# The first normalization of a hybrid encoder block: scaling by diagonal matrices on TensorE, with a fixed TensorE order at the start

## The chip, the cores and the metric

The kernel runs on one core of a Trainium2 chip. The metric is device time in microseconds (us), a median over runs. The engines are named as in the profile: PE is TensorE's matmul, PEld its weight load, DVE is VectorE, ACT is ScalarE, POOL is GpSimd, and SP is the queue that issues most DMAs.

## What is computed

One layer of a hybrid encoder works on 1024 frames of 1024 features, all in float32. The change touches the first of its three parts, and the third part in passing:

```python
x = x + 0.5 * swiglu(rmsnorm(x, ffn1_norm), ffn1_w_gate, ffn1_w_up, ffn1_w_down)   # first FFN, width 2816
h = rmsnorm(x, mix_norm); p = h @ w_in                                             # gMLP and gated DeltaNet
x = x + concat(A, B) @ w_out
x = x + 0.5 * swiglu(rmsnorm(x, ffn2_norm), ffn2_w_gate, ffn2_w_up, ffn2_w_down)   # second FFN
y = rmsnorm(x, final_norm)

rmsnorm(x, g) = x * rsqrt(mean(x * x) + 1e-6) * g        # mean over the 1024 features of a frame
swiglu(x, ...) = (silu(x @ w_gate) * (x @ w_up)) @ w_down
```

## The kernel before

**Precision.** Every operand of a product is split into a rounded high part and a remainder (`split`: ACT makes the high part, DVE or POOL subtracts it from the source), and a product of two split operands is three matmuls (`mm3`: high by high, high by low, low by high).

**Layout.** `x` is loaded in eight tiles of 128 frames (`xs[0]` to `xs[7]`). For the first products the features must lie on the partitions, so that each tile of frames is transposed on TensorE. The hidden width of 2816 is worked through in 22 chunks of 128 columns of the gate and of the up matrix.

**Seven products for eight.** Chunks 1 to 21 (`gu`) multiply 2 by 2 blocks in Winograd's scheme: with the transposed activations as blocks B11, B12, B21 and B22 (frames 0 to 511 or 512 to 1023, features 0 to 511 or 512 to 1023) and their sums T1 to T4, seven products of 12 matmuls each do for eight. The sums T1 to T4 come from DVE and POOL. Chunk 0 (`gu_plain`) uses the plain eight products, since the sums are not there yet. It runs in two halves: 256 columns of frames of each block, then the other 256. In each half it makes 96 matmuls of 256 columns: gate and up, two frame blocks, and two feature blocks of four 128-feature steps `k`.

**The start (`start1`).** For each tile ACT squares and sums, DVE and POOL make the reciprocal root, and DVE scales the tile by it and by the gain `g`, which was broadcast to all partitions by a DMA (`grow`, line 66). TensorE transposes the scaled tile four 128-column pieces at a time into a PSUM bank (`transposed`, line 95), and ACT and DVE take from the bank the high part, the low part and the sums (`blocks`, lines 118 to 150). The first four tiles (0, 4, 1, 5) feed the first half of chunk 0 and the other four (2, 6, 3, 7) the second half. The weight pieces of a chunk come by `load_gu` (SP's queue, line 185), and their sums (line 191) are POOL's.

**Order.** A scheduler orders the instructions of every engine from the program; each engine then works its list strictly in order, and waits where a semaphore is missing. PSUM has two pools of four banks, `mm` (`A`) and `ax` (`X`). In the start the transposes take `ax`, and chunk 0's four accumulators take `mm`. `weight_sums(q)` (line 278) prepares sums of the down matrix for the later product; it is called once every two chunks, from chunk 1 on, and its work is DMA and POOL.

**The second FFN** uses the same `gu_plain`, `gu` and `blocks`. Its norm gain is broadcast by the same `grow`, into one buffer that all four gains share in turn.

Of the kernel before, what the change touches and what calls it, by code (L numbers as in the profile page):

```python
# [17 lines left out]
P = 128  # L18
# [12 lines left out]
def block_kernel(ctx: ExitStack, tc, a, out):  # L31
# [75 lines left out]
    class Combos:  # L107
        def __init__(self, g, qp, bp):
            self.g, self.qp, self.bp, self.B, self.f = g, qp, bp, {}, {}

        def put(self, n, i, src, eng):
# [5 lines left out]
            t = self.B[n][:, :, :, i * P:i * P + P]  # L117
# [34 lines left out]

        def put_sums(self, i, names, engs):
# [11 lines left out]
    def ffn(cb, wgu, wd, ps, rp, gp, qp, bp, start, load_xts, emit, before={}, fill=None):  # L165
# [63 lines left out]
        def gu_plain(sl, b12):  # L229
# [81 lines left out]
        for c in range(1, NCH):  # L311
            together(load_gu(c))
            if c % 2:
                weight_sums(c // 2)
            else:
# [129 lines left out]
    ba = cp.tile([P, 16, 8], F32, tag="ba", name="ba")[:, :8]  # L445
# [9 lines left out]
    xs = load_x(xdram, (0, 4))  # L455
    g = grow("ffn1_norm")
    xs.update(load_x(xdram, (1, 5)))

    with ExitStack() as f1:
# [5 lines left out]
        cb = Combos(g, qp, bp)  # L465

        def start1(f):
            def xi(i):
                return xs[i], xs[i + 4]

            uv = [cb.sums() for _ in range(2)]
            for j in range(2):
                for i in range(2):
                    normed(xi(i)[j], g, xi(i)[j], uv[i][j])
# [3 lines left out]
            weights = f.load_gu(0, True)  # L478
            next(weights)
            xs.update(load_x(xdram, (2, 6, 3, 7)))  # L480
            b = b12()
            parts = [cb.blocks(i, f.X, xi(i), uv[i], b) for i in range(2)]
            together(*parts, n=2)
            together(*parts, weights)
            rest = xi(2) + xi(3)
            ms = sm.tile([P, 4], F32, tag="ssk", name="ms4")
            for i, x in enumerate(rest):
                nc.scalar.activation(f.gtile(F32, "junk").rearrange("p s n -> p (s n)"), x, AF.Square, accum_out=ms[:, i:i + 1])
            rs = sm.tile([P, 4], F32, tag="rk", name="rs4")
            nc.vector.tensor_scalar(rs, ms, 1.0 / D, EPS, op0=ALU.mult, op1=ALU.add)  # L490
            rpow(rs, rs, 4)
            for i, x in enumerate(rest):
                nc.vector.scalar_tensor_tensor(x, x, rs[:, i:i + 1], g, op0=ALU.mult, op1=ALU.mult)
            f.gu_plain(slice(0, 256), b)
            b = b12()
            for i in range(2, 4):
                together(cb.blocks(i, f.X, xi(i), cb.sums(xp), b))
            f.gu_plain(slice(256, 512), b)
            V, G = nc.vector, nc.gpsimd
            together(*(cb.put_sums(i, ("T2", "T1", "T3", "T4"), (V, G, V, G)) for i in range(4)))  # L500
# [42 lines left out]
        ffn(cb, a["f1gu"], a["f1wd"], ps, rp, gp, qp, bp, start1, load_xts, to_mid, {2: [after]}, z0)  # L543
# [14 lines left out]
    with ExitStack() as f2:  # L558
# [37 lines left out]
        cb = Combos(g2, qp, bp)  # L596
# [710 lines left out]
```

## Time and profile before

| | before |
|---|---|
| median of 3 runs | 1849.43 us (1847.9, 1849.43, 1852.1) |
| the profiled execution's own time | 1841.22 us |
| its span, first to last instruction | 1839.4 us |
| PE busy | 1784.1 us, 97% |
| DVE, ACT and POOL busy | 65%, 37%, 41% |
| PE busy from 0 to 60 us | 39.2 us |

The span is what the trace covers; 1.8 us of the profiled execution lie outside it. The profiled execution was faster than the three timed runs by some 8 us, so that differences in the trace are compared with the trace, and carried to the median as differences. A chunk of `gu` takes 84 matmuls of 512 columns. "Busy" of PE is modelled from pipelined matmuls.

### The profile page before, as it was taken

Reading aid. Unit: us, or ns where it says so; the run is one execution under the profiler, and the core shown is the slowest. Engines: PE = TensorE matmul, PEld = TensorE weight load, DVE = VectorE, ACT = ScalarE, POOL = GpSimd, SP = SyncE. Lnnn points to the kernel's source line nnn. Section 1 sums busy time; section 2 is a strip of 40 time slices with the busy share of each in tenths; the row PEclk is TensorE's granted clock in tenths of the full one; section 3 lists DMA queues with packets and bytes.
Section 4 is the critical chain, followed back from the end, with each engine's and each line's share of the span. In section 5 each row is a group of like instructions: output and inputs, shape, how many; then the busy total and the mean of one; then the engine's idle time right before and its main releaser. Section 6 shows DMA issues by size and latency. Waiting matters only on the chain.

```text
span 1839.4 us, 25484 instructions
## 1 busy us (share of the span) xinstructions
PE 1784.1 (97%) x9735; PEld 1524.8 (83%) x9735; DVE 1191.7 (65%) x1531; ACT 686.6 (37%) x1193; POOL 747.9 (41%) x583
## 2 busy tenths in 40 slices
PE   5999999999999999898999999999999999999997
PEld 4888888888788889797788989988888888878886
DVE  6867676665565575769655344587776766656546
ACT  6333332333343454432344533452333323243433
POOL 4667666565140012212132420366666665614001
PEclk9999999999999999999999999999999999999999
DMA  5353443544957445453432254334535445495744
GB/s 196 108 175 136 162 152 134 184 158 163 339 188 258 155 177 164 140 195 100 133 94 67 90 197 136 109 104 165 178 132 171 144 154 188 142 344 185 264 142 149
DMA packets 134441, 302.26 MB, mean 164 GB/s; under 512 B 27408, under 2 KB 42032, under 8 KB 134320
## 3 DMA queue, kind: packets, MB, share of 16 engines
q1 hardware_dynamic: 131824, 296.20, 46.9%
q10 hardware_dynamic: 2496, 4.44, 0.8%
q8 instruction: 76, 1.25, 0.3%
q14 instruction: 45, 0.37, 0.1%
HBM read 208.83 MB, written 91.77 MB: 163 GB/s over the span
## 4 chain that ended last, share of the span: by engine, by line
PE 78%; DVE 8%; DMA 5%; POOL 4%; issue 3%; ACT 2%; SPq 0%; POOLq 0%; DVEq 0%; ACTq 0%
PE mm L53 43%; PE ax L53 32%; POOL s L191 1%; POOL t L278 1%; DMA left<-hq 1%; DVE acc L873 1%; PE ax L95 1%; PE sd L53 1%; DMA graw<-in_f1gu_dram 1%; POOL s L278 1%; PE sc L53 1%; DVE T L119 0%; DVE unit L62 0%; DVE wk L62 0%; DVE E L797 0%
## 5 line engine op out<-in xcount | busy, mean ns | idle before, releaser
L53 PE MATMUL mm<-unit 128*128 128x512 f32 x1056 | 244.9, 392 | 4.2 <-ACT unit L61 2.2
L53 PEld LDWEIGHTS mm<-unit 128*128 128x128 f32 x1056 | 198.8, 189 | 47.4 <-ACT unit L61 3.3
L191 POOL TENSOR_TENSOR s<-graw 128x512 f32<-128x512 f32 x84 | 130.3, 1551 | 262.9 <-DMA graw<-in_f2gu_dram 116.0
L62 DVE TENSOR_TENSOR ga<-graw,ga 128x512 fp32r<-128x512 f32 x134 | 155.9, 1166 | 99.9 <-ACT ga L61 99.2
L61 ACT CAST gs<-s 128x512 fp32r<-128x512 f32 x168 | 104.5, 622 | 301.8 <-PE mm L53 151.0
L62 DVE TENSOR_TENSOR unit<-left,unit 128x1024 fp32r<-128x1024 f32 x84 | 101.9, 1215 | 133.0 <-ACT unit L61 132.3
L53 PE MATMUL ax<-T,gs 128*128 128x512 f32 x792 | 183.1, 389 | 0.0
L53 PE MATMUL ax<-unit 128*128 128x512 f32 x792 | 180.5, 389 | 0.0
L53 PEld LDWEIGHTS ax<-T,gs 128*128 128x128 f32 x792 | 148.7, 188 | 30.8
L53 PEld LDWEIGHTS ax<-unit 128*128 128x128 f32 x792 | 148.7, 188 | 30.8
L62 DVE TENSOR_TENSOR gs<-s,gs 128x512 fp32r<-128x512 f32 x168 | 172.7, 1030 | 2.3
L53 PE MATMUL mm<-B,ga 128*128 128x512 f32 (+1 forms) x864 | 166.8, 347 | 3.3 <-ACT B L118 1.9
L61 ACT CAST unit<-left 128x1024 fp32r<-128x1024 f32 x84 | 82.5, 982 | 230.2 <-PE ax L53 100.5
L53 PE MATMUL mm<-T,gs 128*128 128x512 f32 x720 | 166.5, 389 | 0.0
L53 PEld LDWEIGHTS mm<-B,ga 128*128 128x128 f32 x864 | 139.5, 194 | 23.4 <-ACT B L118 2.5
L53 PEld LDWEIGHTS mm<-T,gs 128*128 128x128 f32 x720 | 135.2, 188 | 28.0
L70 POOL TENSOR_TENSOR rs<-rs,half 128x1 f32<-128x1 f32 (+1 forms) x29 | 19.2, 662 | 334.5 <-DVE rs L76 334.4
L53 PE MATMUL mm<-actT,wk 128*128 128x512 f32 x576 | 150.4, 403 | 0.0
L53 PE MATMUL ax<-B,ga 128*128 128x512 f32 x528 | 127.2, 390 | 1.4 <-DVE ga L62 1.4
L53 PE MATMUL mm<-wk,actT 128*128 128x256 f32 x960 | 123.5, 285 | 2.7 <-DVE wk L62 2.7
L53 PEld LDWEIGHTS mm<-wk,actT 128*128 128x128 f32 x960 | 117.4, 190 | 3.4 <-DVE wk L62 3.0
L53 PEld LDWEIGHTS mm<-actT,wk 128*128 128x128 f32 x576 | 103.6, 188 | 18.8
(239 smaller groups left out, 3046.0 us busy)
## 6 DMA issues: line engine op xcount, KB each, us to landing
left<-hq SPq DMA_DIRECT2D x70, 512.0 KB, 5.0
graw<-in_f1gu_dram SPq DMA_DIRECT2D x44, 512.0 KB, 5.4
wq<-t SPq DMA_DIRECT2D x44, 512.0 KB, 2.8
hq<-s SPq DMA_DIRECT2D x44, 512.0 KB, 3.1
graw<-in_f2gu_dram SPq DMA_DIRECT2D x44, 512.0 KB, 4.7
right<-wq SPq DMA_DIRECT2D x40, 512.0 KB, 4.8
wd<-in_f1wd_dram SPq DMA_DIRECT2D x22, 512.0 KB, 6.6
hq<-sg SPq DMA_DIRECT2D x22, 512.0 KB, 3.7
```

What stands on the lines that cost most here:

```text
L53: nc.tensor.matmul(*args, **kw)
L61: nc.scalar.copy(h, src)
L62: nc.vector.tensor_tensor(l, src, h, op=ALU.subtract)
L70: nc.gpsimd.tensor_tensor(o, i, half[:, :w], op=ALU.pow)
L95: nc.tensor.transpose(ps[:, i * P:(i + 1) * P], blk(i), ident)
L191: nc.gpsimd.tensor_tensor(f, u, v, op=op)
L278: nc.gpsimd.tensor_tensor(o, u, v, op=op)
L873: nc.vector.scalar_tensor_tensor(acc, pad[:, j:j + 512], cw[:, blk, j:j + 1], acc, op0=ALU.mult, op1=ALU.add)
```

## The change

1. **Norm by diagonals.** The tiles are no longer scaled. For each tile ACT squares (now with the scale 1/32 ahead of the square, so that the sum is the mean), POOL adds the epsilon and takes the power, and a 128x128 diagonal matrix `dg` of the tile's 128 factors is made from the identity (on DVE for the first four tiles, on ACT for the other four). TensorE then multiplies a piece of `x` by this diagonal in float32, which transposes and scales at once. The gain is now a column `g1` with one number per partition (a DMA of 32 bytes per partition), and is applied as ACT (`nc.scalar.mul`) and DVE (`scalar_tensor_tensor`) read the bank.
2. **TensorE order fixed.** The start stands under a manual schedule for PE. Ahead of it, 24 float32 products of the identity by itself go into a bank that nobody reads. Bank `c` now holds piece `c` of all four tiles (512 columns), so that a half needs eight banks. `gu_plain` goes step by step in `k`, and the last four banks' products stand between the first four steps. The sums T1 to T4 are cast and subtracted in pieces of 1024 elements per partition instead of 512.
3. **Weight sums later.** `weight_sums(0)` moves from chunk 1 to chunk 2, and chunk 1's weights are loaded within the start.
4. **Broadcast pinned.** The DMA of `grow` keeps its place in the program's order on ACT.

The order of the tiles changes too: 0, 1, 4, 5 and then 2, 3, 6, 7. The diff, cut:

```diff
     def grow(name):
         g = cp.tile([P, D], F32, tag="grow", name="grow")
-        nc.scalar.dma_start(g, a[name].to_broadcast([P, D]))
+        tc.keep_in_program_order(nc.scalar.dma_start(g, a[name].to_broadcast([P, D])))
         return g
...
+        def scaled_blocks(self, i, pp, xts, dg, g, f, b12, ahead):
+            sl = slice(i * 256, i * 256 + 256)
+            t3, t1, t2, t4 = self.f[i] = f
+            def less(o, src, c, v):
+                nc.vector.scalar_tensor_tensor(o, src, g[:, c:c + 1], v, op0=ALU.mult, op1=ALU.subtract)
+            def put(h, l, src, c):
+                nc.scalar.mul(h, src, g[:, c:c + 1])
+                less(l, src, c, h)
+            banks = []
+            def turn(k):
+                cs = range(len(banks), len(banks) + k)
+                banks.extend(bank(*pp) for _ in cs)
+                for n, x in enumerate(xts):
+                    for c in cs:
+                        mm(banks[c][:, n * P:n * P + P], x[:, c * P:c * P + P], dg[:, n * P:n * P + P], start=True, stop=True)
+            turn(ahead)
+            for c in range(8):
+                if c == len(banks):
+                    turn(1)
+                u, v = banks[c][:, :256], banks[c][:, 256:]
+                k = c % 4
+                if c < 4:
+                    b = self.block("B11")
+                    put(b[:, 0, k, sl], b[:, 1, k, sl], u, c)
+                    nc.scalar.mul(t3[:, k], u, g[:, c:c + 1])
+                    b = b12[k // 2]
+                    put(b[:, 0, k % 2], b[:, 1, k % 2], v, c)
+                    less(t1[:, k], v, c, t3[:, k])
+                else:
+                    b = self.block("B21")
+                    put(b[:, 0, k, sl], b[:, 1, k, sl], u, c)
+                    b = self.block("B22")
+                    put(b[:, 0, k, sl], b[:, 1, k, sl], v, c)
+                    less(t2[:, k], v, c, t1[:, k])
+                    less(t4[:, k], u, c, t2[:, k])
+                yield
...
-            for i, x in ((0, "B11"), (1, "B12"), (0, "B21"), (1, "B22")):
-                first = x[1] == "1"
-                for p, wt in ((gates[i], g["B11" if first else "a12"]), (ups[i], g["a21" if first else "a22"])):
-                    products(p, wt, xs[x], sl, first, not first)
+            for first in (True, False):
+                for k in range(4):
+                    for i, x in enumerate(("B11", "B12") if first else ("B21", "B22")):
+                        x = xs[x]
+                        for p, wt in ((gates[i], g["B11" if first else "a12"]), (ups[i], g["a21" if first else "a22"])):
+                            mm3(p, wt[:, 0, k], wt[:, 1, k], x(0, k, sl), x(1, k, sl), first and k == 0, not first and k == 3, skip_group_check=True)
+                    yield
...
+            def factors(ts, diag):
...
+                    nc.scalar.activation(junk, xs[t], AF.Square, scale=D ** -0.5, accum_out=m)
+                    nc.gpsimd.tensor_scalar(r, m, EPS, None, op0=ALU.add)
+                    rpow(r, r, 1)
+                    diag(dg[:, n * P:n * P + P], ident, r)
...
+            def plain(i, dg, fs, b, ahead, also=()):
+                bl = cb.scaled_blocks(i, f.X, [xs[t] for t in order[i]], dg, g1, fs, b, ahead)
+                together(islice(bl, 4))
+                together(also)
+                pr = f.gu_plain(slice(i * 256, i * 256 + 256), b)
+                for _ in bl:
+                    next(pr)
+                together(pr)
+            with tc.manual_schedule(engines={mybir.EngineType.PE}):
+                warm = bank(*f.X)
+                for _ in range(24):
+                    mm(warm[:, :P], ident, ident, start=True, stop=True)
...
+                plain(0, dg, four(cb.sums() + cb.sums()), b12(), 4, weights)
+                dg = factors(order[1], nc.scalar.mul)
+                t4 = rp.tile([P, 1088], F32, tag="graw", name="t4", bufs=4)[:, :D].rearrange("p (a n) -> p a n", a=2)
...
+                plain(1, dg, fs, b12(), 1)
...
+            together(f.load_gu(1), *(cb.scaled_sums(i, ("T2", "T1", "T3", "T4"), (V, G, V, G)) for i in range(2)))
```

**TensorE and DVE between the two halves of chunk 0.** The first two pieces show TensorE's list there, before and then of the change; `mm_...` are chunk 0's accumulators, `ax_...` the `ax` banks, `x_...` the tiles of frames, `dg_395` the diagonals of the second four tiles, and `ga..` weight pieces.

```order
L53 MATMUL mm_262<-B22_227,ga22_240 128x256 x11
L95 MATMUL ax_368<-ident_69,x_156 128x128 x4
L95 MATMUL ax_376<-ident_69,x_158 128x128 x4
L95 MATMUL ax_386<-ident_69,x_156 128x128 x4
L95 MATMUL ax_393<-ident_69,x_158 128x128 x4
L95 MATMUL ax_404<-ident_69,x_160 128x128 x4
L53 MATMUL mm_438<-B11_172,ga11_150 128x256
```

Of the change:

```order
L53 MATMUL mm_258<-B22_250,ga22_239 128x256 x3
L53 MATMUL ax_422<-dg_395,x_180 128x128
L53 MATMUL ax_422<-dg_395,x_182 128x128
...
L53 MATMUL ax_455<-dg_395,x_186 128x128
L53 MATMUL ax_466<-dg_395,x_180 128x128
...
L53 MATMUL ax_466<-dg_395,x_186 128x128
L53 MATMUL mm_477<-B11_214,ga11_171 128x256 x3
```

What moved: the transposes of one pair of tiles filled a bank each and freed it soon; now 16 products fill the four banks `ax_422` to `ax_455`, and the fifth, `ax_466`, takes the memory of `ax_422`, so that it and all that stands behind it wait until ACT and DVE have read `ax_422`. DVE's list at that place, of the change:

```order
L163 SCALAR_TENSOR_TENSOR f_191<-ax_317,ba_76,f_190 128x256
L209 TENSOR_TENSOR T2_624<-f_190,T2_624 128x4x256
L306 TENSOR_TENSOR sg_388<-sg_388,mm_257 128x256
L209 TENSOR_TENSOR T3_643<-f_188,T3_643 128x4x256
L306 TENSOR_TENSOR sg_388<-sg_388,mm_258 128x256
L163 SCALAR_TENSOR_TENSOR B11_214<-ax_422,ba_76,B11_214 128x256
L163 SCALAR_TENSOR_TENSOR B11_214<-ax_433,ba_76,B11_214 128x256
L163 SCALAR_TENSOR_TENSOR B12_420<-ax_422,ba_76,B12_420 128x256
L163 SCALAR_TENSOR_TENSOR f_418<-ax_422,ba_76,f_417 128x256
```

What moved: the low parts of T2 and T3 of the first half now stand ahead of the first reader of `ax_422`, of which the last, `f_418`, frees the bank. Before, the four scalings of tiles (line 493) and two products with `sg` stood there, and the low parts of the sums (line 119) came later.

**ACT and POOL at the same place,** of the change; `f_188` to `f_191` are the sums t3, t1, t2, t4 of the first half, and `rk`, `ssk` the factors.

```order
L546 ACTIVATE dg_395<-ident_69,rk_394 128x128
L208 CAST T1_634<-f_189 128x4x256
L208 CAST T2_624<-f_190 128x4x256
L208 CAST T4_654<-f_191 128x4x256
L305 ACT_TABLE_LOAD
L305 ACTIVATE sg_388<-mm_255 128x256
L208 CAST T3_643<-f_188 128x4x256
L305 ACTIVATE sg_388<-mm_256 128x256
L166 ACTIVATE B11_214<-ax_422,ba_76 128x256
```

POOL's list of the change there:

```order
L70 TENSOR_TENSOR rk_394<-rk_394,half_70 128x1
L209 TENSOR_TENSOR T1_634<-f_189,T1_634 128x4x256
L206 TENSOR_TENSOR f_188<-f_190,f_188 128x1024
L209 TENSOR_TENSOR T4_654<-f_191,T4_654 128x4x256
L209 TENSOR_TENSOR T1_634<-f_418,T1_634 128x4x256
```

What moved: ACT's cast of T3 stands ahead of its first reading of `ax_422`, and needs `f_188`, which POOL makes only after T1's low part. Before, ACT's first reading of a bank there (`f_366<-ax_368`) stood behind casts of pieces of 512 elements.

**ACT in the second FFN, ahead of the bank readings of its second half,** before:

```order
L118 CAST T4_11029<-f_10281 128x4x128
L66 DMA grow_11338<-in_final_norm_dram 128x1024
L243 ACT_TABLE_LOAD
L243 ACTIVATE sg_10837<-mm_10737 128x256
L243 ACTIVATE sg_10837<-mm_10738 128x256
L133 COPY f_10844<-ax_10846 128x512
```

Of the change:

```order
L121 CAST T4_11084<-f_10336 128x4x128
L305 ACT_TABLE_LOAD
L305 ACTIVATE sg_10892<-mm_10792 128x256
L305 ACTIVATE sg_10892<-mm_10793 128x256
L136 COPY f_10899<-ax_10901 128x512
```

What moved: the broadcast of the last gain, which waits for the last reader of the gain before it, leaves this place, and stands 52 instructions later.

## Rows read from the trace of the kernel before

**Rows 1.** The page's forty slices, busy share of PE in tenths.

```profile
PE   5999999999999999898999999999999999999997
```

**Rows 2.** Windows: stretch, length, busy PE PEld DVE ACT POOL, clock, DMA, GB/s.

```profile
0.00:60.00 60.00, 39.16 (x251) 35.87 (x252) 45.43 (x60) 37.06 (x72) 30.43 (x28) 0.89 0.43 162
30.00:40.00 10.00, 4.86 (x35) 4.48 (x34) 6.50 (x5) 4.47 (x10) 7.24 (x6) 0.84 0.15 52
40.00:50.00 10.00, 7.30 (x32) 6.23 (x31) 9.55 (x17) 7.02 (x15) 4.42 (x4) 0.50 0.37 130
50.00:60.00 10.00, 10.00 (x83) 10.00 (x83) 10.00 (x11) 5.72 (x12) 8.67 (x6) 0.98 0.12 45
```

**Rows 3.** Chain of waits, 0 to 170 us: start, length, what.

```profile
62.67 18.89 PE ax L53 x82
...
81.56 19.04 PE mm L53 x84
```

**Rows 4.** PE's timeline: start, time, engine, line, operation, tiles, shape, count, [idle before, releaser].

```profile
9.36 1.11 PE L95 MATMUL ax<-ident,x 128*128 128x128 f32 x4 [9.36 <-DVE x L82]
...
22.84 1.04 PE L95 MATMUL ax<-ident,x 128*128 128x128 f32 x8
...
36.26 0.63 PE L95 MATMUL ax<-ident,x 128*128 128x128 f32 x4 [3.56 <-DVE x L493]
38.47 2.79 PE L95 MATMUL ax<-ident,x 128*128 128x128 f32 x12 [1.58 <-DVE x L493]
...
45.87 2.80 PE L95 MATMUL ax<-ident,x 128*128 128x128 f32 x12 [0.28 <-DVE B L142]
...
50.78 1.48 PE L53 MATMUL mm<-B,ga 128*128 128x256 f32 x11
...
912.67 1.05 PE L53 MATMUL ax<-wq,ks 128*128 128x128 f32 x8
```

**Rows 5.** Groups by line and shape: count, busy us, mean ns, idle before.

```profile
L53 PE MATMUL ax<-wq,ks 128*128 128x128 f32 x64 | 8.6, 275 | 0.0
...
L95 PE MATMUL ax<-ident,oh 128*128 128x128 f32 x32 | 5.0, 280 | 0.0
...
L61 ACT CAST unit<-left 128x1024 fp32r<-128x1024 f32 x70 | 73.7, 1053 | 189.9 <-PE ax L53 79.9 <-PE mm L53 67.9 <-DMA left<-hq 31.0
...
L70 POOL TENSOR_TENSOR rs<-rs,half 128x1 f32<-128x1 f32 x28 | 18.1, 649 | 334.5 <-DVE rs L76 334.4
```

**Rows 6.** DMA issues, 0 to 24 us: KB each, us to landing.

```profile
ident<-in_cst_dram ACTq DMA_DIRECT2D x1, 64.0 KB, 4.0
```

**Rows 7.** One window of 1 us, columns as in rows 2.

```profile
3.00:4.00 1.00, 0.00 (x0) 0.00 (x0) 0.00 (x0) 0.00 (x0) 0.00 (x0) 1.00 1.06 414
```

**Rows 8.** ACT's timeline, 0 to 10 us.

```profile
0.72 0.40 ACTq L454 DMA_DIRECT2D ident<-in_cst_dram  x1
...
4.56 1.06 ACT L74 ACTIVATE f<-x 128x1024 f32<-128x1024 f32 x1 [1.64 <-DMA x<-in_x_dram]
```

**Rows 9.** DVE's timeline, 38 to 44 us.

```profile
40.64 0.74 DVE L244 TENSOR_TENSOR sg<-sg,mm 128x256 f32<-128x256 f32 x2
```

**Rows 10.** Instructions on tile graw, 0:70 us: ns min/median/max, first/last start.

```profile
L62 DVE TENSOR_TENSOR ga<-graw,ga x8: 681/1541/1780, 15.4 to 69.8; 128x512 fp32r<-128x512 f32 x8
L191 POOL TENSOR_TENSOR s<-graw x4: 1292/1459/1743, 26.1 to 67.0; 128x512 f32<-128x512 f32 x4
```

**Rows 11.** PE's timeline, 1184 to 1201 us (second FFN's start).

```profile
1185.04 1.84 PE L53 MATMUL mm<-B,ga 128*128 128x256 f32 x14
1187.53 2.90 PE L53 MATMUL mm<-B,ga 128*128 128x256 f32 x22 [0.66 <-DVE ga L62]
```

**Rows 12.** ACT's timeline, 1192 to 1201 us.

```profile
1197.47 1.28 ACT L243 ACT_TABLE_LOAD   x1 [4.73 <-DVE xn L82]
1198.77 0.66 ACT L243 ACTIVATE sg<-mm 128x256 f32<-128x256 f32 x2
1199.31 0.59 ACT L133 COPY f<-ax 128x512 f32<-128x512 f32 x1
```

More of the change, by code (lines that the diff above doesn't have):

```diff
@@ L116, in put @@
                     self.B[n] = act_tile(name=n)
-            t = self.B[n][:, :, :, i * P:i * P + P]
+            return self.B[n]
+        def put(self, n, i, src, eng):
+            t = self.block(n)[:, :, :, i * P:i * P + P]
             nc.scalar.copy(t[:, 0], src)
@@ L163, in together, with ffn @@
             pass
-    def ffn(cb, wgu, wd, ps, rp, gp, qp, bp, start, load_xts, emit, before={}, fill=None):
+    def ffn(cb, wgu, wd, ps, rp, gp, qp, bp, start, load_xts, emit, before={}, fill=None, late=0):
         A, X = (ps[0], "mm"), (ps[1], "ax")
@@ L311, in ffn @@
         for c in range(1, NCH):
-            together(load_gu(c))
-            if c % 2:
+            if c not in gu_s:
+                together(load_gu(c))
+            if c % 2 and c > late:
                 weight_sums(c // 2)
-            else:
+            elif c % 2 == 0:
+                if c // 2 * 2 == late + 1:
+                    weight_sums(0)
                 hidden_sums(c // 2 - 1)
@@ L444, in block_kernel @@
     sp = {n: dr.tile([8, P, 512], F32, tag="sp" + n, name="sp" + n) for n in "zvm"}
-    ba = cp.tile([P, 16, 8], F32, tag="ba", name="ba")[:, :8]
+    ba = cp.tile([P, 16, 8], F32, tag="ba", name="ba")
+    g1 = ba[:, 8]
+    ba = ba[:, :8]
     def load_x(src, ts):
@@ L475, in b12 @@
             def b12():
                 return [f.gtile(F32R, "B12").rearrange("p s (k n) -> p s k n", k=2) for _ in range(2)]
[L478 to L498, printed above, removed]
+            def four(ts):
+                return [t.rearrange("p a (b n) -> p (a b) n", b=2) for t in ts]
+            def plain(i, dg, fs, b, ahead, also=()):
[6 more added lines that the diff above has]
+                together(pr)
@@ new lines, in start1 @@
+            with tc.manual_schedule(engines={mybir.EngineType.PE}):
+                warm = bank(*f.X)
+                for _ in range(24):
+                    mm(warm[:, :P], ident, ident, start=True, stop=True)
+                weights = f.load_gu(0, True)
+                dg = factors(order[0], nc.vector.tensor_scalar_mul)
+                together(islice(weights, 2))
+                xs.update(load_x(xdram, order[1]))
+                plain(0, dg, four(cb.sums() + cb.sums()), b12(), 4, weights)
+                dg = factors(order[1], nc.scalar.mul)
+                t4 = rp.tile([P, 1088], F32, tag="graw", name="t4", bufs=4)[:, :D].rearrange("p (a n) -> p a n", a=2)
+                fs = four([xp.tile([P, 2, 512], F32, tag="x", name="f") for _ in range(3)] + [t4])
+                plain(1, dg, fs, b12(), 1)
@@ L626, in start2 @@
                     normed(xs[i + 4 * j], g2, xns[i][j])
-            f.gu_plain(slice(0, 256), b)
+            together(f.gu_plain(slice(0, 256), b))
             c = b12()
@@ L630, in start2 @@
                 together(cb.blocks(i, pp, xns[i], cb.sums(xp), c))
-            f.gu_plain(slice(256, 512), c)
+            together(f.gu_plain(slice(256, 512), c))
             V, G = nc.vector, nc.gpsimd
```

42 lines of the change are left out of this document (25 added, 17 removed).

## The prediction

> **What bounds the kernel now.** The first view is the page's forty slices: PE stands at 9 nearly everywhere, and only the first slice, of 46 us, is at 5 [rows 1]. So time can be won where PE is not full. The windows measure it: 39.2 us of work in the first 60 [rows 2]. The chain of waits gives the frame: from 62.67 us it is PE alone, one chunk every 19.04 us, and chunk 1 ends at 81.56 [rows 3]. Whatever the start gains must show as an earlier end of chunk 1; nothing behind it has slack to give.
>
> PE's timeline names the waits: the largest is from 32.7 to 36.26 for the scaling of the tiles on DVE (line 493), with 1.58 for the same line behind it [rows 4]. The clock costs too: the granted clock is 0.84 in 30 to 40 us, 0.50 in 40 to 50 and 0.98 in 50 to 60, that is 1.2 GHz from 3.2 us before 40 to 0.4 behind 50, 36.8 to 50.4 [rows 2]. Pace shows it: a transpose takes (1.04-0.27)/7 = 0.11 us at 22.84, and (2.79-0.42)/11 = 0.215 at 38.47 [rows 4]. The transposes at 9.36 take 1.11 for four, the slow pace too, against 0.63 at 36.26 [rows 4]. So the start is at 1.2 GHz before the change as well.
>
> **The price of a diagonal.** A float32 product that is no transpose stands in the trace as two records: the program issues 32 of `ax<-wq,ks` and the trace has 64, but of `ax<-ident,oh` it issues 32 and has 32 [rows 5]. Eight records take 1.05 us, (1.05-0.275)/7 = 0.11 each [rows 4], so that a diagonal product costs 0.22 us at 2.4 GHz where a transpose cost 0.11, and 0.43 at 1.2. The Trainium skill ("TensorE: Matmul & The Clock Gate", Terms) says of the transpose mode that it is 4 times faster for float32; by that a diagonal product would take 0.44 us, and the sum below would be 14 us longer ahead of what waits hide. I go by the rows, which have a factor of 2; rival 4 is the other case. The work of PE in the start is then 64 x 0.223 + 192 x 0.12 = 37.3 us after the 24 idle products; before it was 64 x 0.11 + 23 = 30. The 0.12 is that of eleven records at 50.78, (1.48-0.28)/10 [rows 4].
>
> **The start, step by step** (us from the span's start).
>
> *Factors.* The first tile lands at 4.5 [rows 8], and the DMAs move some 414 GB/s, 0.5 MB in 1.27 us [rows 7]. Without the broadcast of 0.5 MB the other three of the first half land by 4.5 + 3 x 1.27 = 8.3. Its square takes 1.06 [rows 8], POOL's power 0.65 [rows 5] and the add no more than that, the diagonal 0.3 on DVE (a quarter of the 0.68 of 512 columns [rows 10], and its start): the fourth diagonal is ready at 11.0 at the latest.
>
> *Idle products.* The identity lands 4.0 us after its issue [rows 6] at 0.72 [rows 8], at 4.7. 24 products at 0.43 would end at 15.0. After 36.8 the clock rose 4.5 us into the run of work that began at 45.87; so I let it rise at 9.3: 11 products before, 13 at 0.22 after, end 12.2. So it is these, not the factors, that set the first diagonal: 12.2, and 16 products fill four banks at 15.8, the first one at 15.1.
>
> *First drain.* Bank 0 needs ACT's high part (0.38), two weight casts that stand between (0.52 each, half of 1024 columns [rows 5]), t3 and B12; on DVE B11's low part, two weight low parts (0.6 each), B12's low part and t1. One 256-column reading follows the next after 0.28 on ACT (two in 0.66 [rows 12]) and 0.33 on DVE (two in 0.74 [rows 9]). That ends at 18.3; PE waits 2.5 us. Then four banks and the first 48 products, 16 x 0.223 + 48 x 0.12 = 9.35, and 48 more, 5.8: the first half ends at 33.4 (before: 32.7). ACT's squares of the last four tiles lie beside that, and DVE, with 28 readings of 0.33, keeps ahead.
>
> *Second drain.* 16 diagonals to 37.0, then `ax_466` waits for `ax_422`. ACT's chain: the last diagonal at 30.1 (square at 27.9, POOL 0.75), cast of T1 to 31.2; POOL then T1's low part and `f_188`, 2.5 us each alone (two pieces of 1.29 [rows 10], less a start); ACT casts T3 (1.05 [rows 5]); DVE T3's low part (1.2 alone), then one `sg` and four readings: 40.2. Beside each other both engines slow down: 512 elements on DVE take 0.68 alone and 1.78 beside POOL, on POOL 1.29 and 1.74 [rows 10]. With that from 32.2 on it is 42.4. The Trainium skill ("SBUF — State Buffer", Who interferes with whom) has the shared port of DVE and POOL as a lock: with two inputs in SBUF the later one waits for the whole other instruction. By that DVE would wait out three POOL instructions, and it would be 42.8; the rows agree with the size, and no run here tells a lock from a shared rate. I take 41.5, nearer the row of the pair, since most of this stretch has both at work: PE idles 4.5 us.
>
> *Second half.* 9.35 + 5.8 = 15.1 at 2.4 GHz: 56.6. A pause of 3.6 us was followed by the fall at 36.8, so I let the clock fall, and rise 4.5 us after work resumes: half of 4.5 is lost, 58.9.
>
> *Chunk 1.* Its second product needs T2's and `gs2`'s low parts. The last bank is filled 7.2 us before 58.9, eight DVE readings and a cast later T2 begins at 55.6 and ends at 56.8 alone or 59.1 beside POOL, `gs2` at 57.4 or 60.9; needed at 61.6. So no wait, and 84 x 0.227 = 19.04 ends it at 77.9. For some ten handovers from engine to engine at 0.06 each I add 0.6: 78.5 against 81.56, **3.0 us less**.
>
> **The other parts.** The first weight sums, four POOL pieces, move behind chunk 1; there POOL takes its sums for chunk 1 instead, so that I count them at nothing. Were POOL's list as full as before there, DVE's pieces would cost 1.78 for 0.68 each [rows 10], which is rival 2. In the second FFN the step-wise `gu_plain` asks for `ga21` after 3 products, not 12: PE had done 14 products when it waited for that low part until 1187.53 [rows 11], and will have done 5: 9 x 0.12 = 1.1 us more wait. The pinned broadcast pays it back: ACT stood still for 4.73 us, with that DMA's wait in its list (the order ahead of these rows), so that table load and `sg` came only at 1197.47; the first bank was read at 1199.31 [rows 12]. Without it the reading needs only its transposes, which come 0.6 later: 1199.1. What PE waits for next hangs on that reading. I count 0, bounds -0.4 and +1.1. The other orders move one DMA or two copies, with full PE over them: 0.
>
> **Sum.** -3.0 us: the trace's 1841.2 becomes 1838.2, and on the scale of the runs 1849.4 becomes 1846.4, 0.16% less. What a measurement of this kernel tells from no change is about 0.2%, 3.7 us.
>
> **Rivals.**
> 1. *The second drain is short and the clock holds.* T1 and T3 on POOL run alone (40.2), no fall, and the idle products end at 11.5: 58.9-2.25-1.3-0.7 = 54.7, chunk 1 ends at 73.7 to 76: 5 to 8 us less, 1841.4 to 1844.4. For it: POOL's shortest pieces are at 1.29, and DVE's at 0.68 [rows 10]. Against: the T2 and T3 pieces have both inputs in SBUF, as `ga` there.
> 2. *DVE bounds chunk 1.* If POOL is busy through 56 to 70, T2, `gs2`, `gs1`, T3 and `gs3` take 3.5+1.78+1.78+3.5+1.78 with two `sg` of 0.33 between, from 55.6 to 68.6 or, with a weight piece of chunk 2 between, 70; PE asks at 67.1. Chunk 1 ends at 80 to 81.5: 0 to 1.5 us less, 1848 to 1849.4. For it: DVE was the last wait before, at 62.67 [rows 3]. Against: POOL's pieces of chunk 2 need a weight load that stands behind `sg`'s store in SP's queue and takes the buffer of `t4`; until it lands POOL has little to do.
> 3. *Slower: the clock does not rise by the idle products.* Then these end at 15.0, the first bank is full 13 x 0.43 later, the first drain ends at 23.8, and with a rise 4.5 us after that the first half ends at 41.2, 7.8 later than above. Nothing behind it takes that up: chunk 1 ends at 86, 4.8 us more, 1854. It decides with the time of the rise: at 15 the gain is gone, at 25 the kernel is slower by 3.7. For it: at 9.36 to 15, before, PE ran at the slow pace with work of a microsecond at a time. Against: there it paused in between, and here it has no pause from 4.7 on.
> 4. *Slower: four passes instead of two.* At 0.44 us a diagonal product the 64 put 14 us more on PE, of which the two drains hide some 5: 6 us more than before, 1855. Against: eight records in 1.05 us. The Trainium skill ("TensorE: Matmul & The Clock Gate", Terms) has the factor of 4 that would make this so; the trace does not agree.
>
> **How the numbers follow.** Forecast (1.2 to 4.9 us less) 0.43, rival 1 0.26, rival 2 0.18, rival 3 0.08, rival 4 0.02, an unseen wait of either sign 0.03. A third of the forecast lies beyond 3.7 us: faster 0.14+0.26+0.02 = 0.42; slower 0.08+0.02+0.01 = 0.11; the same 0.47. The forecast's own range is 1844.5 to 1848.2. For 8 in 10, rival 1's end, with 1 us for the spread of the runs, gives 1840.5, and rival 2 with the upper run gives 1852.
>
> **What would show it.** In the trace after: 24 pairs of records of the identity from 4.7; their pace changing at about 9.3; first diagonal near 12.2; a wait of 2.5 us at 15.8 for DVE; a wait of 3 to 5.5 us at 37 for DVE behind T3; granted clock 0.5 for some us after it; chunk 1 ending near 78.5. The prediction is wrong if the start has another long wait, if the clock never rises before 16, or if chunk 2 waits for its weights.

## The result and the profile after

The change made the kernel slower. The median of 6 runs is 1856.88 us (1855.47 to 1863.87) against 1847.91 of the kernel before (6 runs, 1847.65 to 1852.1): ratio 1.0046, 95% interval 1.0028 to 1.0064, that is 5 to 12 us more. The forecast was 3 us less, in a range of 1840.5 to 1852.0.

The profiled execution took 1857.08 us, with a span of 1854.9. The span shown of before was 1839.4, so the traces differ by 15.5 us and the medians by 9.0. The profiled execution of before was a quick one; experiment 1 shows how much executions of one kernel differ.

The chain of waits of the kernel after, 0 to 120 us (columns as in [rows 3]):

```profile
64.47 2.49 POOL T L209
66.98 3.80 DMA graw<-in_f1gu_dram
...
75.63 0.69 DVE pe L326
...
82.10 19.04 PE mm L53 x84
```

Chunk 1 ends at 82.10, against 81.56 in [rows 3] and 78.5 forecast. So the start gained nothing, and it is no longer the product of weights that is last there, but a chain over POOL, a weight load and DVE, inside chunk 1. The page's forty slices have a 6 where [rows 1] have a 5: PE does more in the first slice, and is not done sooner.

PE's timeline of the kernel after, the start:

```profile
4.91 7.20 PE L53 MATMUL ax<-ident 128*128 128x128 f32 x48 [4.91 <-DMA ident<-in_cst_dram]
11.95 3.74 PE L53 MATMUL ax<-dg,x 128*128 128x128 f32 x32
18.35 1.92 PE L53 MATMUL ax<-dg,x 128*128 128x128 f32 x8 [2.66 <-DVE f L163]
...
27.78 7.44 PE L53 MATMUL mm<-B,ga 128*128 128x256 f32 x60
35.06 3.73 PE L53 MATMUL ax<-dg,x 128*128 128x128 f32 x32
45.60 2.05 PE L53 MATMUL ax<-dg,x 128*128 128x128 f32 x8 [6.81 <-DVE f L163]
...
76.36 3.02 PE L53 MATMUL ax<-B,gs 128*128 128x512 f32 x12 [0.17 <-DVE pe L326]
...
81.94 2.88 PE L53 MATMUL mm<-B,ga 128*128 128x512 f32 x12
```

32 records of diagonal products take 3.74 us, 0.117 each, so the price of a diagonal is as forecast. The two drains are 2.66 and 6.81 us (forecast 2.5 and 4.5). Behind each of them eight records take some 2 us, twice the 1.06 that they take later. The windows say the same: the granted clock is 0.92, 0.90 and 0.66, which is 1.6, 2.0 and 6.8 us at 1.2 GHz (for about half of the 6.8 us PE stands idle). The slow pace of the identity's first records shows in their times alone: over them the granted clock of the windows reads 1.00.

```profile
10.00:20.00 10.00, 7.34 (x60) 7.18 (x59) 5.18 (x13) 5.21 (x13) 0.65 (x2) 0.92 0.84 325
20.00:30.00 10.00, 10.00 (x80) 10.00 (x79) 6.65 (x16) 7.78 (x20) 2.35 (x6) 0.90 0.19 62
40.00:50.00 10.00, 4.40 (x24) 4.43 (x25) 7.40 (x14) 6.24 (x16) 1.86 (x1) 0.66 0.00 1
```

The second drain, in POOL's timeline of the kernel after, and then DVE's:

```profile
33.89 2.38 POOL L209 TENSOR_TENSOR T<-f,T 128x1024 fp32r<-128x1024 f32 x1 [1.45 <-ACT T L208]
36.23 3.33 POOL L206 TENSOR_TENSOR f<-f 128x1024 f32<-128x1024 f32 x1
39.53 2.34 POOL L209 TENSOR_TENSOR T<-f,T 128x1024 fp32r<-128x1024 f32 x1
```

```profile
34.79 2.56 DVE L209 TENSOR_TENSOR T<-f,T 128x1024 fp32r<-128x1024 f32 x1 [1.52 <-ACT T L208]
...
40.67 2.28 DVE L209 TENSOR_TENSOR T<-f,T 128x1024 fp32r<-128x1024 f32 x1 [2.81 <-ACT T L208]
42.87 0.41 DVE L306 TENSOR_TENSOR sg<-sg,mm 128x256 f32<-128x256 f32 x1
43.20 0.86 DVE L163 SCALAR_TENSOR_TENSOR B<-ax,ba,B 128x256 fp32r<-128x256 f32 x2
```

T1's low part, then the difference for T3 (`f`), then T3's cast on ACT, then on DVE T3's low part (40.67), and only then DVE reads the bank that PE waits for. POOL's row at 39.53 is T4's low part, DVE's at 34.79 T2's.

The second FFN, PE's timeline of the kernel after; [rows 11] have its counterpart:

```profile
1193.89 0.76 PE L53 MATMUL mm<-B,ga 128*128 128x256 f32 x5
1196.66 1.33 PE L53 MATMUL mm<-B,ga 128*128 128x256 f32 x9 [2.01 <-DVE ga L62]
1199.70 11.49 PE L53 MATMUL mm<-B,ga 128*128 128x256 f32 x82 [1.71 <-DVE x L672]
1211.04 1.91 PE L95 MATMUL ax<-ident,xn 128*128 128x128 f32 x16
...
1230.68 2.68 PE L53 MATMUL ax<-B,ga 128*128 128x512 f32 x11
```

Of the kernel before, behind the two rows of [rows 11]:

```profile
1190.58 7.46 PE L53 MATMUL mm<-B,ga 128*128 128x256 f32 x60 [0.15 <-DVE x L593]
1197.88 1.91 PE L95 MATMUL ax<-ident,xn 128*128 128x128 f32 x16
...
1218.10 2.91 PE L53 MATMUL ax<-B,ga 128*128 128x512 f32 x12
```

From the first product to the first transpose it is now 17.15 us; before it was 12.84 (1185.04 to 1197.88). The second wait was not in the forecast: behind 14 products PE asks for the fourth accumulator's bank, which DVE has not yet emptied (line 672, before 593, adds a bank of the product with `w_out` to `x`). Before, PE asked for it behind 36 products. In both kernels the bank is there 5.5 to 5.8 us after the first product (1190.58 and 1199.70), so the order costs the products that are not done by then, and the first wait lies within the second. The clock adds to it: the granted clock is 0.58 in 1199 to 1202 us and 0.85 in 1202 to 1205, which is 3.4 us at 1.2 GHz, and 1.00 there in the kernel before.

### The profile page after: what moved, and what is told of

Read it like the earlier page. It is cut to its first block, busy times and chain, and to the rows that moved or that the text cites. A ratio compares the mean times of both kernels' runs of the same rounds, so it can differ in the third digit from the quotient of the medians.

```text
span 1854.9 us, 25735 instructions
## 1 busy us (share of the span) xinstructions
PE 1800.2 (97%) x9847; PEld 1541.8 (83%) x9847; DVE 1127.6 (61%) x1542; ACT 690.3 (37%) x1205; POOL 747.3 (40%) x588
## 4 chain that ended last, share of the span: by engine, by line
PE 81%; DVE 5%; POOL 5%; DMA 4%; issue 2%; ACT 2%; SPq 0%; POOLq 0%; DVEq 0%; ACTq 0%
PE mm L53 46%; PE ax L53 32%; POOL s L250 1%; DMA left<-hq 1%; POOL t L340 1%; DVE acc L952 1%; PE ax L95 1%; PE sd L53 1%; PE sc L53 1%; POOL T L209 1%; POOL s L340 1%; POOL E L878 0%; DVE o L82 0%; DVE unit L62 0%; POOL brs L70 0%
## 5 line engine op out<-in xcount | busy, mean ns | idle before, releaser
L62 DVE TENSOR_TENSOR ga<-graw,ga 128x512 fp32r<-128x512 f32 x134 | 132.3, 990 | 122.8 <-ACT ga L61 122.5
L62 DVE TENSOR_TENSOR gs<-s,gs 128x512 fp32r<-128x512 f32 x168 | 167.4, 998 | 5.7 <-ACT gs L61 3.2
L70 POOL TENSOR_TENSOR rs<-rs,half 128x1 f32<-128x1 f32 x24 | 16.0, 665 | 323.4 <-DVE rs L76 323.3
```

What stands on the lines that cost most here:

```text
L62: nc.vector.tensor_tensor(l, src, h, op=ALU.subtract)
L70: nc.gpsimd.tensor_tensor(o, i, half[:, :w], op=ALU.pow)
```

## The experiments

Theory A: the step order in the second FFN makes some 4 us of the loss, the start is held by the chain of the second drain, and the rest differs from execution to execution. Rival B: the whole loss comes from the start, or from the stages in the middle, by the change. All ratios are to the kernel before, run on the same chip. "Chunk 2" is the start of PE's first product of chunk 2, "drain" the second drain, "FFN 2" the time there from the first product to the first transpose; all from PE's timelines.

| run | chunk 2 | drain | FFN 2 | ratio (95%) |
|---|---|---|---|---|
| before | 81.40 | | 12.84 | 1 |
| 1 before, again | 81.39 | | 12.90 | 1.0013 (0.9992 to 1.0034) |
| after | 81.94 | 6.81 | 17.15 | 1.0046 (1.0028 to 1.0064) |
| 2 after, again | 81.78 | 6.82 | 17.07 | one execution |
| 3 after, FFN 2 old | 82.89 | 6.81 | 12.92 | 1.0021 (1.0005 to 1.0036) |
| 4 before, FFN 2 new | 81.26 | | 16.95 | 1.0015 (0.9996 to 1.0034) |
| 5 = 3, T3 behind | 78.86 | 1.72 | 12.94 | 0.9975 (0.9955 to 0.9995) |
| 6 = 5, idle products in the first drain | 78.77 | 1.72 | 12.92 | 0.9973 (0.9949 to 0.9997) |
| 7 = 3, no idle products | 77.20 | 2.78 | 12.90 | one execution |
| 8 = 3, weight sums at chunk 1 | 91.34 | 6.82 | 12.96 | one execution |
| 9 = 6, reading ahead of gs | 75.73 | 1.72 | 12.88 | 0.9985 (0.9956 to 1.0014) |
| 10 = 9, 8 idle products | 71.88 | 1.46 | 13.14 | 0.9966 (0.9945 to 0.9987) |
| 11 = 10, two gs behind | 69.81 | 1.44 | 13.16 | 0.9983 (0.9965 to 1.0001) |
| 12 = after, 8 idle products | 75.28 | 3.24 | 17.10 | 0.9992 (0.9974 to 1.001) |

**1 and 2. Both kernels again,** unchanged.

> The kernel before, unchanged, profiled a second time. Theory A: some 6 us of the 15.5 us between the two profiled spans (1839.4 and 1854.9) belong to executions, not to the change, above all the one sum of E on POOL at 739 us that took 9.17 us in the trace after and 1.53 in the one before, and PE's clock falls at waits; then this span is 1844 to 1849, and 6 or 7 us of the gain in the trace lie in the mixing stage and at the two joints of the FFNs. Rival B: all 15.5 us come from the change; then this span is 1839 to 1841, with that piece at 1.5 us again. Ratio 0.999 to 1.001 by both.

> The changed kernel, unchanged, profiled a second time. Theory A: the start (chunk 1 ends at 82.1) and the second FFN's start (17.1 us from its first product to its first transpose, against 12.8 before) come out within 0.5 us of the first trace, while the mixing stage and the joints can differ by some us; span 1849 to 1856. Rival B: everything repeats within 1 us, the 9.17 us piece on POOL too, span 1854 to 1856.

The second span of before is 1847.4, 8 us above the first; that of after is 1853.1, 1.8 below. The start, and the second FFN up to its first transpose, repeat within 0.2 us in both kernels. What differs is elsewhere, above all around one piece on POOL: the row of the kernel after, then that of before in its second execution.

```profile
738.98 9.17 POOL L878 TENSOR_TENSOR E<-csa,grb 128x512 f32<-128x512 f32 x1 [3.89 <-DMA grb<-grd]
```

```profile
735.14 8.96 POOL L799 TENSOR_TENSOR E<-csa,grb 128x512 f32<-128x512 f32 x1 [4.10 <-DMA grb<-grd]
```

In the first execution of before it took 1.53, in the second of after 1.35. So it comes with the execution, whatever the kernel. From the start of this piece to the second FFN's first product, four of the five executions with a short piece take 449.4 to 451.2 us and the eight with a piece of 9 us 452.4 to 457.6; run 3, with a short piece and 459.8 us, shows that it is not the only cause. Theory A holds in this, and the differences of the two traces in that stretch are no effect of the change. The one time of run 2, 1855.16 us, is 5.5 us above the median of before on that chip (1849.65), so that the 9.0 us of the medians may be on the high side.

**3 and 4. The second FFN alone.** In 3 its chunk 0 goes back to the old order, in 4 the kernel before gets the new order and the pinned broadcasts.

```diff
-            together(f.gu_plain(slice(0, 256), b))
+            together(f.gu_plain(slice(0, 256), b, False))      # 3: block by block, as before; its other half likewise
```

> The changed kernel with the second FFN's chunk 0 in the old order (gate and up block by block, not step by step); the start stays new. Theory A (the step order there asks for the low part of ga21 and for the third and fourth bank before they are there): 3.5 to 4 us faster than the changed kernel, ratio to before 1.0024 to 1.0034, waits of 0.7 and 0.2 us at the place where 2.01 and 1.71 stood. Rival B (that place costs nothing net; the start or the stages in the middle make the loss): as the changed kernel, ratio 1.004 to 1.005.

> The kernel before with the second FFN's chunk 0 in the new step order and the pinned broadcasts; the start stays old. Theory A: 3.3 to 4 us slower than before, ratio 1.0018 to 1.0022, with waits of 2 and 1.7 us ahead of the third and fourth bank. Rival B: no change, ratio 0.9995 to 1.0005. Rival C (the pins and the order gain what was forecast for them): 0.9998 or less.

PE's timeline of run 3, then of run 4:

```profile
1200.84 1.84 PE L53 MATMUL mm<-B,ga 128*128 128x256 f32 x14
1203.41 10.51 PE L53 MATMUL mm<-B,ga 128*128 128x256 f32 x82 [0.73 <-DVE ga L62]
1213.76 1.91 PE L95 MATMUL ax<-ident,xn 128*128 128x128 f32 x16
```

```profile
1191.67 1.34 PE L53 MATMUL mm<-B,ga 128*128 128x256 f32 x9 [1.79 <-DVE ga L62]
1194.72 11.52 PE L53 MATMUL mm<-B,ga 128*128 128x256 f32 x82 [1.71 <-DVE x L600]
```

The two waits go and come with the order, on either start: 4.1 to 4.2 us. 2.8 of it are the 22 products, at 0.126 us, that PE has not done when the bank comes, and 1.0 is the clock: the last 82 products take 11.49 and 11.52 us with the new order, 10.51 in run 3. From the transposes on to chunk 1 the executions with the new order take 19.6 to 19.7 us; those with the old one and the pinned broadcast take 18.3 where the clock holds (runs 3, 9, 10 and 11) and 19.6 to 19.7 where it falls (5 to 8); before, without the pin, took 20.22 where it fell and 19.08 in run 1, where it held. By the times nothing is settled, since the interval of 4 includes 1 and those of 3 and after overlap; it is the rows that settle it. Theory A is right, with a size a little too small, and rival B is out as far as it has this place cost nothing.

**5 and 6. The second drain, and the clock in the first.** In 5 the cast and the low part of the first half's T3 are issued behind the fourth bank of the second half (`a3` and `o` are ACT's and DVE's last reading of it). In 6 there are ten idle products more, in the first drain.

```diff
+                behind = self.last if (i, n) == (0, "T3") else ()
+                with ExitStack() as order:
+                    for ins in behind:
+                        order.enter_context(tc.issue_after(ins.ins))
                     nc.scalar.copy(t[:, 0], src)
                     eng.tensor_tensor(t[:, 1], src, t[:, 0], op=ALU.subtract)
...
             turn(ahead)
+            for _ in range(idle):                # 6 alone: 10
+                mm(spare[:, :P], ident, ident, start=True, stop=True)
```

> As the run with the second FFN in the old order (e3), and in the start the first half's T3 is cast and its low part taken behind the fourth bank of the second half. Theory A (the second drain of 6.8 us is the chain T1 on POOL, T3's difference, T3's cast, T3's low part, ahead of the bank readings): the drain falls to 1.5 to 2.5 us, the clock does not fall there, and chunk 2 begins at 76 to 78 instead of 81.9; ratio to before 0.998 to 1.0. Rival B (DVE bounds chunk 1: what the drain gives, a wait for T3 or the weight sums inside chunk 1 takes): chunk 2 begins at 80 to 82, with a new wait behind 62; ratio as e3, 1.001 to 1.003.

> As e5, with ten more products of the identity by itself between the first four banks and the fifth, where PE waits 2.66 us. Theory A (that pause makes the clock fall from 18.5 to 21.9, 1.7 us lost): no fall there, the first half ends 1.5 us sooner, chunk 2 begins 1 to 1.7 us before e5. Rival B (the first half is paced by DVE's readings, so the lost clock is hidden): no change of over 0.3 us.

PE's timeline of run 5 with a row of run 6 behind it, then DVE's and POOL's of run 5:

```profile
41.51 1.13 PE L53 MATMUL ax<-dg,x 128*128 128x128 f32 x8 [1.72 <-DVE f L163]
...
73.28 3.01 PE L53 MATMUL ax<-B,gs 128*128 128x512 f32 x12 [2.84 <-DVE pe L342]
```

```profile
71.62 4.56 PE L53 MATMUL ax<-B,gs 128*128 128x512 f32 x12 [2.85 <-DVE pe L344]
```

```profile
71.54 1.09 DVE L62 TENSOR_TENSOR gs<-s,gs 128x512 fp32r<-128x512 f32 x1 [3.73 <-ACT gs L61]
72.55 0.68 DVE L342 TENSOR_TENSOR pe<-ax,pe 128x512 f32<-128x512 f32 x1
```

```profile
60.91 3.35 POOL L215 TENSOR_TENSOR T<-t,T 128x1024 fp32r<-128x1024 f32 x1 [0.93 <-ACT T L214]
68.20 1.29 POOL L256 TENSOR_TENSOR s<-graw 128x512 f32<-128x512 f32 x1 [3.95 <-DMA graw<-in_f1gu_dram]
```

Theory A is right on the drain (1.72 us, and no fall behind it), and half right on the gain: chunk 1 begins 6.7 us sooner than in run 3 (56.66 against 63.34), and 2.7 of that come back in chunk 1, as a wait of 2.84 for 0.17. Chunk 2, at 78.86, begins between the two expectations. Read upward: PE waits for DVE's reading `pe`; that stands behind the low part of a sum for chunk 2; that waits for POOL's sums, these for a weight load, and the load for the buffer that `t4` holds until POOL has made T4's low part at 64.26. In run 6 the clock holds through the first drain and PE reaches chunk 1's second product 1.67 us sooner (57.73 against 59.40), as theory A has it. The reading `pe` comes as much sooner (70.89 against 72.55), and so does the product behind it (71.62 against 73.28). But chunk 2 begins as in 5, since the clock falls at that wait in run 6 alone: the granted clock is 0.50 in 72 to 74 us, where run 5 has 1.00, and the 12 products take 4.56 us for 3.01. Why two waits of 2.84 and 2.85 us end in different clocks is not shown.

**7. No idle products** (`range(24)` becomes `range(0)`).

> As e3 without the 24 idle products at the start. Theory A (they raise the clock at 8.3 us and cost nothing but a microsecond): the first diagonals begin at 9 to 11 at 1.2 GHz, 0.43 us each, the first four banks are full at 16 to 18, the clock rises later, and chunk 2 begins 2 to 4 us later than in e3. Rival B (the clock rises at the diagonals as soon): chunk 2 begins within 0.5 us of e3, or up to 1 us sooner.

```profile
8.45 6.69 PE L53 MATMUL ax<-dg,x 128*128 128x128 f32 x32 [8.45 <-DVE dg L556]
17.76 1.95 PE L53 MATMUL ax<-dg,x 128*128 128x128 f32 x8 [2.62 <-DVE f L163]
```

Both expectations were wrong. Chunk 2 begins 5.7 us sooner than in 3, not later. The diagonals keep the slow pace, 0.21 us a record, for all of their 6.69 us, and are done at 15.1; behind the idle products, at 0.117, they are done at 16.3 in run 3 (12.60 + 3.74). The rest of the gain is not the clock's: without the idle products the scheduler wrote POOL's list another way, with T1's low part already within the first half, at 22.27, so that the difference for T3 starts at 31.20 instead of 36.85 (run 3), and the second drain is 2.78 instead of 6.81. This run alone doesn't part the two.

**8. The weight sums at chunk 1,** as before (the argument `late`, which moves them, is 0).

> As e3 with the first weight sums at chunk 1 again, as in the kernel before. Theory A (the move costs and gains nothing): the start within 0.3 us of e3, and the wait ahead of the first down product 3 to 3.5 us, as after. Rival B (POOL is full in chunk 1, so the move was needed): PE waits in chunk 1 or 2 for gs or T4, 2 to 6 us. Rival C (the move is what lengthened the wait ahead of the first down product from 1.3 to 2.0 us to 3.1 to 3.4): that wait is 1.2 to 2.0 again.

PE's timeline of run 8, then POOL's:

```profile
83.98 4.80 PE L53 MATMUL ax<-B,gs 128*128 128x512 f32 x12 [7.03 <-DVE pe L336]
```

```profile
64.27 3.46 POOL L350 TENSOR_TENSOR t<-wd 128x512 f32<-128x512 f32 x2
67.68 3.98 POOL L350 TENSOR_TENSOR t<-wd,t 128x512 f32<-128x512 f32 x2
71.62 2.84 POOL L209 TENSOR_TENSOR T<-t,T 128x1024 fp32r<-128x1024 f32 x1
```

Rival B is right, and by more: chunk 2 begins 8.45 us later than in 3. The four pieces hold up T4's low part, with it the buffer, the load (the sum that waits for it starts at 78.95, in run 3 at 71.95) and chunk 1's reading. So in the new start the move of the weight sums is worth 8 us; the start of before has no load behind `t4`. The wait ahead of the first product with the down matrix is 3.4 us, so rival C is out.

**9, 10 and 11. The load's chain taken off the path, and fewer idle products.** In 9 the low part of chunk 2's `s2` stands behind chunk 1's second reading on DVE; 10 has 8 idle products at the start; in 11 `s1` and `s2` stand behind the third reading.

```diff
                 t = gtile(F32R, "g" + n)
-                split(t[:, 0], t[:, 1], src)
+                with ExitStack() as order:
+                    if (c, n) == (2, "s2"):
+                        order.enter_context(tc.issue_after(hid["read"]))
+                    split(t[:, 0], t[:, 1], src)
...
-                for _ in range(24):
+                for _ in range(8):               # 10 and 11
                     mm(warm[:, :P], ident, ident, start=True, stop=True)
```

> As e6, and on DVE the low part of chunk 2's first sum (gs of s2) stands behind chunk 1's second bank reading (pe). Theory A (chunk 1's wait of 2.85 us is DVE's order: that low part waits for a weight load which waits for T4 to leave its buffer, and the reading that PE waits for stands behind it): the wait at 71.6 goes, the clock does not fall there, and chunk 2 begins at 74 to 74.8 instead of 78.8; ratio 0.994 to 0.996. Rival B (the wait only moves: PE then waits as long in chunk 2 for gs or T4, or at pe for another reason): chunk 3 begins within 1 us of e6, 97 to 98; ratio as e6, 0.997.

> As e9 with 8 idle products at the start instead of 24. Theory A (24 are too many: they run at 1.2 GHz till the clock rises and keep PE until 12 us while the factors are there at 8.5): the diagonals begin at 8.5 to 9, at first at 1.2 GHz, the first four banks are full at 13.5 to 14.5 instead of 16.4, and chunk 2 begins 1 to 2 us sooner than e9. Rival B (the first half is then paced by the weights' casts and DVE's readings): chunk 2 begins within 0.5 us of e9. Rival C (the clock rises late or falls again in the first pause): chunk 2 begins 1 to 3 us later.

> As e10, with the low parts of chunk 2's first two sums behind chunk 1's third reading (up) on DVE instead of one behind the second. Theory A (the 1.77 us left in chunk 1 are those two low parts ahead of that reading): the wait goes, chunk 2 begins at 70.0 to 70.3 instead of 71.9; ratio 0.1% below that of e10 (0.9966), not to be told from it by the times. Rival B (PE then waits for them in chunk 2): chunk 3 begins at 90.5 to 91, as e10.

PE's timeline of run 9, then of run 10:

```profile
72.87 3.02 PE L53 MATMUL ax<-T,ga 128*128 128x512 f32 x12 [1.75 <-DVE up L351]
```

```profile
4.79 3.60 PE L53 MATMUL ax<-ident 128*128 128x128 f32 x16 [4.79 <-DMA ident<-in_cst_dram]
8.42 3.84 PE L53 MATMUL ax<-dg,x 128*128 128x128 f32 x32
```

In 9 the wait at the second reading goes, 1.75 us of it come back at the third (between A and B), and in 11 it is gone: 2.1 us, to 69.81, a little more than expected. In 10 the 16 records of the identity end as the factors are there, and the diagonals run at 0.12 us from their start: the clock rose no later for it, at some 8.6 us by the pace, and in 11 and 12 by 8.8. That is not so in every execution: in the seven with 24 idle products the change of pace lies between 8.2 and 10.9 us (an estimate from the time of the 48 records, at 0.213 and 0.117 each), and in run 7 the slow pace lasted to the last diagonal at 15.1. So what 8 products give was seen in three executions in which the clock rose early. Chunk 2 begins 3.85 us sooner than in 9, about twice what was expected. By the times 10 is 0.3% faster than before, the interval of 11 reaches 1, and the two can't be told apart; their starts are 9.5 and 11.6 us shorter than that of before, of which the times show a part only.

**12. The change with 8 idle products,** and nothing else.

> The changed kernel with 8 idle products instead of 24, and nothing else (the second FFN's step order stays new). Theory A (the forecast counted them as the cover of the first diagonal, but 16 of them only hold PE back): the diagonals begin at 8.4 to 9 instead of 11.95, and chunk 2 begins 3 to 5 us before after's 82.0; second FFN as after, 17.1 us to its first transpose; ratio 1.002 to 1.003. Rival B (what is gained ahead is lost in the second drain or in chunk 1, behind T4's buffer): chunk 2 begins at 80 to 82.

PE's timeline of run 12, then POOL's:

```profile
8.40 3.93 PE L53 MATMUL ax<-dg,x 128*128 128x128 f32 x32
...
39.04 1.78 PE L53 MATMUL ax<-dg,x 128*128 128x128 f32 x8 [3.24 <-DVE f L163]
```

```profile
29.25 2.42 POOL L206 TENSOR_TENSOR f<-f 128x1024 f32<-128x1024 f32 x1 [0.40 <-DVE f L163]
31.63 6.62 POOL L209 TENSOR_TENSOR T<-f,T 128x1024 fp32r<-128x1024 f32 x2
```

Chunk 2 begins 6.7 us sooner than in after, where theory A had 3 to 5, and with ratio 0.9992 the loss no longer shows: the start is 6.1 us shorter than before, the second FFN still 4.3 us longer. 3.55 us come from PE's earlier diagonals (8.40 for 11.95). The other 3 lie in the second drain (3.24 for 6.81), where POOL's list now has the difference ahead of T1's low part: the number of idle products changed that list as well.

## Why the prediction was wrong

Three steps failed: the second FFN's "I count 0, bounds -0.4 and +1.1" (it cost 3.7 to 4.8 us), the terms of the second drain (45.6 for 41.5), and the parts in between that were counted at 0 (some 3 us).

**Right.** The frame (chunk 1's end tells the start's gain), the price of a diagonal, the first diagonal (12.2 forecast, 11.95 measured), the four banks (15.8, 15.69), the first drain (2.5, 2.66), the clock's rise: 48 records in 7.20 us at 0.213 and 0.117 each are some 16 slow ones, so it rose at about 8.4 (9.3 forecast). Some of this is luck: over the seven executions with 24 idle products the rise lies between 8.2 and 10.9, and the first diagonal between 11.86 and 12.97. Rivals 3 and 4 are out, and so is rival 1, since the second drain was longer than forecast and the clock fell in both.

**The second FFN, step "I count 0, bounds -0.4 and +1.1".** This is the largest miss. The step priced one of two waits: it followed PE to the low part of `ga21` and stopped. The next thing that PE asks for in the new order is the fourth accumulator's bank. It is there 5.5 to 5.8 us after the first product in either order, and PE has done 14 products by then instead of 36; the other 22 x 0.126 = 2.8 us are the cost, and the 1.1 of the forecast lies within them. The clock, which falls at this wait, adds 1.0: together 3.8 of the 4.1 to 4.3 us (experiments 3 and 4). What the pin gives back is 0.7 (18.33 against 19.08 in experiment 1, both with the clock held) or 0.6 (19.6 against 20.22, both with the clock fallen), less than the 1.1 that was set against it.

**The second drain, 41.5 in the forecast, 45.6 measured.** The mechanism was right, the terms were too small. Against the 40.2 of the terms alone, POOL's chain begins 2.7 us later (33.89 for 31.2), the difference on POOL took 3.33 and not 2.5, T3's low part 2.28 and not 1.2, and from DVE's first reading to PE's next product it took 2.4 us (43.20 to 45.60), with a wait for ACT between, where four readings of 0.33 were counted. Of the late begin 1.8 us are the first half, which ended at 35.2 instead of 33.4, since the clock fell in the first drain; the forecast let the clock fall at the second alone (experiment 6 shows 1.67 us for the first). The 1.3 us that it added for POOL and DVE side by side cover less than the rest. The rows also tell the lock from the shared rate, which the forecast left open: T1's low part on POOL takes 2.38 us with DVE's T2 begun beside it, and T2's ends 1.1 us behind T1's; the difference ends 2.2 us behind T2's, and T3's low part 1.1 behind POOL's T4 (41.87). Each is about as long as it takes alone (1.21 in run 5, 2.42 in run 12), counted from the other engine's end. Experiment 5 shows the chain: moved, the drain is 1.72.

**The parts in between.** From chunk 2 to the start of the POOL sum shown in experiment 1, the three executions with the old start (before, 1 and 4) take 652.4 to 654.2 us, and the eleven with the new one 654.9 to 658.2, 3.3 more on average. The forecast had "I count them at nothing" for the weight sums and 0 for the other orders, without a row of that stretch. 1.4 us of it lie ahead of the first product with the down matrix, where PE waits 1.8 to 3.6 us with the new start and 1.3 to 2.0 with the old one. The pins are not the cause, since run 4 has them; the cause stays open. Run 8, with the weight sums where they were, does not take it away (657.1).

**The idle products.** The forecast saw that they, not the factors, set the first diagonal, and did not ask what fewer would give: 3.5 us where the clock rises early (experiments 10 and 12).

**Chunk 1.** Rival 2 had the right place and the wrong cause. The forecast named the load behind `t4` as a reason why POOL would be idle; it is itself what DVE's list, and so PE, waits for. In the changed kernel it ties with PE to 0.17 us, and so a gain ahead of it counts only as far as this chain moves too: in part in 5 (chunk 1 begins 6.7 us sooner than in 3, POOL's sum behind the load 3.75, at 68.20 for 71.95), and in full in 7 and 12, where POOL's list moved along and the wait stayed at 0.2. In 6 the chain moved by all of the 1.66 us, and the clock took them back. That the move of the weight sums cost nothing in chunk 1 was right (experiment 8).

**What adds up.** Start 0.5, the parts in between 2.8 in the two first traces, second FFN from its first product to chunk 1 3.7 to 4.8 (36.79 against 33.06 in the first execution of before, where the clock fell behind the transposes, and 31.98 in experiment 1, where it held): 7.0 to 8.1 of 9.0 us, and the rest lies within the interval. The loss in between is also one reason why the times of 10 and 11 show less than their starts.

## What to carry to other kernels

When an order of products changes, write down for each engine what is asked for next, and next again, with the time at which it is there: operand, then bank. Here idle products paid until the operands were there and not a record longer. In a kernel whose lists a scheduler writes their number moves other engines' work as well, so compare the lists after each such number. Before a stall is removed, look for what is late next; here a buffer lent to a temporary tied a weight load, three engines and the next chunk together.

## What was not expected of the hardware

One POOL sum of 512 elements, in a stage that the change does not touch, took 8.96 to 9.33 us in eight of the fourteen profiled executions, 5.12 in one (run 11), and 1.35 to 1.55 in the other five. DVE's timeline of the kernel after, beside it:

```profile
738.56 1.28 DVE L876 TENSOR_TENSOR E<-grb,gc 128x512 f32<-128x512 f32 x2
...
745.79 1.21 DVE L62 TENSOR_TENSOR wk<-raw,wk 128x1024 fp32r<-128x1024 f32 x1
```

POOL's sum began at 738.98, and DVE ran one instruction with two inputs in SBUF after the other, twelve of 0.68 us and the one of 1.21, until 747.0; POOL ended 1.15 us later. So DVE did not slow down beside POOL, as it does in [rows 10], but by these rows kept it out for a dozen instructions in a row. In the first execution of before, where the sum took 1.53 us, it was DVE that was slower: two of its instructions took 2.38 us in place of 1.28. The Trainium skill ("SBUF — State Buffer", Who interferes with whom) has the port as a lock that the first to start gets for a whole instruction; the rows agree, and add that the other need not get its turn between two of them.
